# Up projection of a feed-forward block: seven products of half blocks in place of eight for nineteen of twenty-two pairs of tiles

## The chip, the core and the metric

The kernel runs on one core of a Trainium2 chip. TensorE (PE) multiplies, PEld is its weight load, VectorE is DVE, ScalarE is ACT, GpSimd is POOL, and SyncE (SP) issues nearly all DMAs. The metric is the device time of one execution in microseconds; a lower time is better. Before the change the median of three runs is 3589.12 us (3586.46 to 3591.07).

## What is computed

The reference is one layer of an encoder, applied to two batches of 1024 tokens by 1024 features with the same weights. Its last part, which the change touches for the second batch, is a gated feed-forward block with a convolution of width three along the tokens:

```python
D_MODEL = 1024; SEQ = 1024; D_FF = 2816
def _conv_ffn(x, l, prm):
    h = x @ prm['ffn_up'][l]                       # (1024, 1024) @ (1024, 5632)
    cw = prm['conv_w'][l]
    h = cw[0] * _shift_prev(h) + cw[1] * h + cw[2] * _shift_next(h) + prm['conv_b'][l]
    gate, up = jnp.split(h, 2, axis=-1)
    return (jax.nn.gelu(gate, approximate=False) * up) @ prm['ffn_down'][l]

x = _layer_norm(ALPHA * x + _conv_ffn(x, l, prm), prm['ln2_g'][l], prm['ln2_b'][l])
```

Everything before it in the layer (the input projection, the two head groups, the output projection and its norm) is the same before and after.

## The kernel before

Each fp32 operand is split into a high part (`hi`, a rounded copy that ACT makes) and a low part (`lo`, the difference, by POOL for weights and by DVE for activations), and a product of two operands is three matmuls: hi by hi, hi by lo, lo by hi. A matmul multiplies a 128x128 block of weights with 512 tokens and adds to one bank of PSUM.

The normalised input of the feed-forward block stands transposed in `xh` and `xl` (feature block k of 8, 1024 tokens). `phase_f1` runs over 22 pairs j. A pair is two tiles of 128 output features, the gate tile `j` and the up tile `KF + j`. For one tile `weights` loads 512 KB of weights (SP, tile `w`), splits them (`split`: two ACT copies at line 248, four POOL subtractions at line 251 into a second `w`), and `dense` issues 2 halves of the tokens x 8 feature blocks x 3 matmuls (lines 264 to 266) into a PSUM tile `d` of two banks; there are two such tiles, taken in turn. Then ACT applies the middle tap and the bias (line 1068), DVE adds the other two taps (lines 1069 and 1071). With both tiles of a pair there, ACT applies the gelu (line 1074), DVE multiplies (line 1075), and ACT and DVE split the result into `h` (lines 307 and 308).

For the second batch the first half of the tokens of `h` stays in SBUF, in the tile `h`; the second half goes to DRAM and is read back. `phase_f2` multiplies `h` with the down projection: for each half of the tokens and each half of the output features, 22 blocks k x 4 tiles of tokens x 3 matmuls (`dense_t`, lines 288 to 290).

All engines execute in the order of their own queue and wait for semaphores. A scheduler makes these orders from the order of the code, at build time. The tiles come from pools with a fixed number of buffers (`BUFS`: 4 of `w`, 2 of `whi`, 7 of `t`; 2 of the PSUM tile `d`); an instruction that takes a buffer over waits for the last reader of its former content.

## Time and profile before

| what | value |
|---|---|
| median of three runs | 3589.12 us |
| the profiled execution's own time | 3581.8 us |
| its span in the profile | 3580.1 us |
| TensorE busy over the span | 3207.8 us (90%) |
| DVE, ACT and POOL busy over the span | 54%, 38%, 36% |
| up projection of the second batch | about 2838 to 3314 us of the span |
| down projection of the second batch and the last norm | from 3314 us to the end |

The page gives the busy time of each engine over the whole program. The two stages of the table are read from windows of the trace, from timelines of single engines, and from the groups of instructions by line.

### The profile page before, as it was taken

Reading aid. Unit: us, or ns where it says so; the run is one execution under the profiler, and the core shown is the slowest. Engines: PE = TensorE matmul, PEld = TensorE weight load, DVE = VectorE, ACT = ScalarE, POOL = GpSimd, SP = SyncE. Lnnn points to the kernel's source line nnn. Section 1 sums busy time; section 2 is a strip of 40 time slices with the busy share of each in tenths; the row PEclk is TensorE's granted clock in tenths of the full one; section 3 lists DMA queues with packets and bytes.
Section 4 is the critical chain, followed back from the end, with each engine's and each line's share of the span. In section 5 each row is a group of like instructions: output and inputs, shape, how many; then the busy total and the mean of one; then the engine's idle time right before and its main releaser. Section 6 shows DMA issues by size and latency. Waiting matters only on the chain.

```text
span 3580.1 us, 56015 instructions
## 1 busy us (share of the span) xinstructions
PE 3207.8 (90%) x21477; PEld 2543.4 (71%) x21477; DVE 1948.3 (54%) x3550; ACT 1360.1 (38%) x2318; POOL 1299.1 (36%) x1387
## 2 busy tenths in 40 slices
PE   5787877998999986798999999988997899999997
PEld 4566655776778874666778787766875688888876
DVE  6377873345557866888544434356685733333022
ACT  3243432443245643454344343324454433332222
POOL 5265441101322345544211112363352622222464
PEclk9898888998999987888999999989999999999999
DMA  5568875443455655676643336566662322222652
GB/s 163 164 205 228 217 193 142 139 111 112 132 170 162 218 199 152 169 184 163 143 128 111 111 109 219 195 225 196 189 193 86 112 78 76 71 71 73 227 173 86
DMA packets 603359, 545.59 MB, mean 152 GB/s; under 512 B 205340, under 2 KB 477964, under 8 KB 603092
## 3 DMA queue, kind: packets, MB, share of 16 engines
q1 hardware_dynamic: 536532, 508.44, 46.9%
q10 hardware_dynamic: 66560, 33.56, 3.9%
q8 instruction: 171, 2.80, 0.3%
q14 instruction: 96, 0.79, 0.1%
HBM read 361.49 MB, written 180.39 MB: 151 GB/s over the span
## 4 chain that ended last, share of the span: by engine, by line
PE 61%; DVE 14%; DMA 10%; issue 4%; ACT 4%; POOL 4%; SPq 3%; ACTq 0%; DVEq 0%; POOLq 0%
PE d L264 10%; PE d L266 10%; PE d L265 10%; PE s L722 8%; PE d L288 5%; PE d L289 5%; PE d L290 5%; SPq L79 3%; DVE Ntmp L619 2%; DVE N L621 2%; POOL w L251 2%; PE s L917 1%; PE s L918 1%; PE s L942 1%; DMA ab<-AB 1%
## 5 line engine op out<-in xcount | busy, mean ns | idle before, releaser
L251 POOL TENSOR_TENSOR w<-w,whi 128x256 fp32r<-128x256 f32 (+1 forms) x800 | 758.6, 976 | 1271.8 <-ACT whi L248 1117.8
L264 PE MATMUL d<-xh,whi 128*128 128x512 f32 (+1 forms) x2112 | 858.7, 407 | 15.0 <-DVE t L399 6.0
L266 PE MATMUL d<-xh,w 128*128 128x512 f32 (+1 forms) x2112 | 848.5, 402 | 2.3 <-POOL w L251 2.3
L265 PE MATMUL d<-xl,whi 128*128 128x512 f32 (+1 forms) x2112 | 845.4, 400 | 0.6 <-DVE xl L308 0.6
L248 ACT ACTIVATE whi<-w 128x512 fp32r<-128x512 f32 (+1 forms) x536 | 308.0, 622 | 730.1 <-PE d L290 259.5
L264 PEld LDWEIGHTS d<-xh,whi 128*128 128x128 f32 (+1 forms) x2112 | 405.9, 192 | 107.1 <-issue 7.5
L266 PEld LDWEIGHTS d<-xh,w 128*128 128x128 f32 (+1 forms) x2112 | 405.5, 192 | 98.9 <-POOL w L251 3.7
L265 PEld LDWEIGHTS d<-xl,whi 128*128 128x128 f32 (+1 forms) x2112 | 405.7, 192 | 93.3 <-issue 3.3
L1069 DVE SCALAR_TENSOR_TENSOR t<-d,cols,t 128x1023 f32<-128x1023 f32 x88 | 112.8, 1282 | 444.4 <-ACT t L1068 444.4
L288 PE MATMUL d<-whi,xh 128*128 128x512 f32 x640 | 261.8, 416 | 38.2 <-DVE t L1049 21.7
L289 PE MATMUL d<-w,xh 128*128 128x512 f32 x640 | 262.9, 411 | 5.8 <-POOL w L251 5.8
L290 PE MATMUL d<-whi,xl 128*128 128x512 f32 x608 | 247.2, 407 | 0.0
L1049 DVE SCALAR_TENSOR_TENSOR t<-t,d 128x512 f32<-128x512 f32 x112 | 72.7, 680 | 259.5 <-PE d L290 252.4
L926 ACT ACTIVATE e<-e,ms 128x1024 f32<-128x1024 f32 x128 | 146.9, 1148 | 125.4 <-DVE ms L924 105.8
L933 POOL TENSOR_SCALAR e<-e,ms 128x512 f32<-128x512 f32 x128 | 87.6, 698 | 264.5 <-DVE ms L931 122.6
L288 PEld LDWEIGHTS d<-whi,xh 128*128 128x128 f32 x640 | 124.8, 195 | 75.9 <-DVE t L1049 14.1
L289 PEld LDWEIGHTS d<-w,xh 128*128 128x128 f32 x640 | 125.4, 196 | 36.4 <-POOL w L251 8.9
L722 PE MATMUL s<-G,BK 64*128 64x128 f32 x1024 | 110.6, 306 | 35.5 <-DMA Tt<-td 17.8
L290 PEld LDWEIGHTS d<-whi,xl 128*128 128x128 f32 x608 | 118.2, 194 | 27.7
L917 PE MATMUL s<-k,qh 128*128 128x512 f32 x256 | 113.3, 444 | 25.5 <-DVE ms L920 16.5
L619 DVE TENSOR_TENSOR Ntmp<-N 128x30 f32<-128x30 f32 (+14 forms) x240 | 115.6, 482 | 36.5 <-DMA N<-abd 31.5
L737 DVE TENSOR_TENSOR G<-s,ms 64x256 f32<-64x256 f32 x128 | 53.5, 418 | 144.3 <-PE s L722 143.1
(226 smaller groups left out, 5748.9 us busy)
## 6 DMA issues: line engine op xcount, KB each, us to landing
w<-in_ffn_up SPq DMA_DIRECT2D x88, 512.0 KB
w<-in_ffn_down SPq DMA_DIRECT2D x88, 512.0 KB
h<-t SPq DMA_DIRECT2D x66, 512.0 KB
ab<-AB ACTq DMA_DIRECT2D x64, 512.0 KB
w<-in_w_in SPq DMA_DIRECT2D x58, 512.0 KB
G<-ab SPq DMA_DIRECT2D x128, 128.0 KB
BK<-ab SPq DMA_DIRECT2D x64, 256.0 KB
w<-in_w_out SPq DMA_DIRECT2D x32, 512.0 KB
```

What stands on the lines that cost most here:

```text
L248: nc.scalar.activation(out=hi[:, s], in_=w[:, s], func=AF.Copy)
L251: nc.gpsimd.tensor_tensor(out=lo[:, s], in0=w[:, s], in1=hi[:, s].bitcast(F32), op=ALU.subtract)
L264: nc.tensor.matmul(o, wh, rh, start=first, stop=False)
L265: nc.tensor.matmul(o, wh, rl, start=False, stop=False)
L266: nc.tensor.matmul(o, wl, rh, start=False, stop=last)
L288: nc.tensor.matmul(out[i], lh, wh, start=k == ks[0], stop=False)
L289: nc.tensor.matmul(out[i], lh, wl, start=False, stop=False)
L290: nc.tensor.matmul(out[i], ll, wh, start=False, stop=k == ks[-1])
L619: nc.vector.tensor_tensor(out=tv, in0=N[:, 0:j, j : j + 1].to_broadcast([P, j, w]), in1=N[:, j : j + 1, j + 1 : 32].to_broadcast([P, j, w] ...
L722: last = self.nc.tensor.matmul(*args, **kw)
L917: nc.tensor.matmul(pp, q_[0], k_[c][:, ks], start=True, stop=False)
L926: nc.scalar.activation(out=e_, in_=e_, func=AF.Exp, bias=ms[:, 2 + c : 3 + c], accum_out=ms[:, 4 + c : 5 + c])
```

## The change

For the pairs 3 to 21 of the second batch the two tiles of a pair are computed together. The weights of a pair are four half blocks: `a11` and `a12` are the feature blocks 0 to 3 and 4 to 7 of the gate tile, `a21` and `a22` those of the up tile. The tokens are two halves as well, so that four quarter results (`c11`, `c12` for the gate tile, `c21`, `c22` for the up tile) are two products of half blocks each, eight in all. Winograd's form of Strassen's scheme needs seven products of sums instead. Each of these is 4 feature blocks x 3 matmuls.

* `right` makes the sums of the activations once, in tiles `T1`, `T2`, `T4` (and a fourth sum over the second half of the tokens of blocks 0 to 3 in `xh` and `xl` themselves), during the pairs 0 to 2, which still take eight products.
* `seven` loads a pair's weights, makes four sums `s1` to `s4` on DVE, splits seven half blocks (a copy on ACT and a subtraction on POOL each), and issues the seven products. Their order on TensorE is enforced (`issue_after(self.turn)`): s1, a11, then the last product (a22) of the pair before, then s2, a12, s4, s3.
* Between the products three copies on ACT move partial results (`es` from `e`; `c12` from `c11`; `c21` from `c12`, lines 1183, 1184, 1187), and two additions on DVE add `es` (line 1152).
* All of `h` of the second batch goes to DRAM, and `phase_f2` reads all of it back, into the buffers of the sums and of `xh` and `xl`, as half as large transfers.

The core of the diff (parts of `phase_f1` that only move into functions are left out):

```diff
-            def pre(k):
+            def pre(k, n):
+                if n:
+                    return
...
-            self.dense_t(w, 512 * n, ks, lhs, range(4 * g, 4 * g + 4), put, n, pre if n == 0 else None, last and n == 1)
...
+            self.dense_t(w, 512 * n, ks, lhs, range(4 * g, 4 * g + 4), put, n, lambda k: pre(k, n), last and n == 1)
...
+        def eight(m):
+            ws = self.weights(I["ffn_up"][0], m * P, KT)
+            pp = self.dpsum()
+            self.dense(pp, ws, rhs, (0, 1), KT)
+            return pp
...
+        def gated(j, gate, up):
+            nc.scalar.activation(out=gate, in_=gate, func=AF.Gelu)
+            nc.vector.tensor_tensor(out=up, in0=gate, in1=up, op=ALU.mult)
             for half in range(2):
-                stay = keep is not None and half == 0
-                o = keep[:, j] if stay else self.dt("t", F32R, shape=(P, 2, 512))
-                self.hilo(gu[1][:, 512 * half : 512 * half + 512], o[:, 0], o[:, 1])
-                if not stay:
-                    self.ld(out=S["h"][j][half], in_=o)
-
-    def phase_f2(self, b, out, keep=None):
+                o = self.dt("t", F32R, shape=(P, 2, 512))
+                self.hilo(up[:, 512 * half : 512 * half + 512], o[:, 0], o[:, 1])
+                self.ld(out=S["h"][j][half], in_=o)
+
...
+        if tl is None:
+            for j in range(KF):
+                gated(j, *(conv(eight(m), m) for m in (j, KF + j)))
+            return None
+        right, early = self.right(tl), 3
+        for j in range(early):
+            pps = [eight(m) for m in (j, KF + j)]
+            if j == 0:
+                next(right)
+            if j == early - 1:
+                blocks = next(right)
+            gated(j, conv(pps[0], j), conv(pps[1], KF + j))
+        self.turn = None
+        last = None
+        for j in range(early, KF):
+            this = self.seven(tl, j, blocks)
+            next(this)
+            if last:
+                gated(j - 1, gate, conv(next(last), KF + j - 1))
+            gate, last = conv(next(this), j), this
+        gated(KF - 1, gate, conv(next(last), 2 * KF - 1))
+        return blocks
+
+    def right(self, tl):
+
+
+        nc = self.nc
+        xh, xl = self.xT
+        block = lambda a, b: [tuple(x[:, 4 * a + k, 512 * b : 512 * b + 512] for x in (xh, xl)) for k in range(4)]
+        T = [tl(f"T{i}", dt=F32R, shape=(P, 4, 2, 512)) for i in (1, 2, 4)]
+        op = lambda out, a, b, o: nc.vector.tensor_tensor(out=out, in0=a, in1=b, op=o)
+        at = lambda a, b, k: [x[:, 4 * a + k, 512 * b : 512 * b + 512].bitcast(F32) for x in (xh, xl)]
+        one = lambda: tl("S", 4)
+        for k in range(4):
+            b11, b12, b21, b22 = (at(a, b, k) for a in range(2) for b in range(2))
+            t1, u = one(), one()
+            op(t1, b12[0], b11[0], ALU.subtract)
+            nc.gpsimd.tensor_tensor(out=u, in0=b12[1], in1=b11[1], op=ALU.subtract)
+            op(t1, t1, u, ALU.add)
+            for n, b in ((0, None), (1, b22), (2, b21)):
+                if b:
+                    op(t1, b[0], t1, ALU.subtract)
+                    op(t1, t1, b[1], ALU.add)
+                self.hilo(t1, T[n][:, k, 0], T[n][:, k, 1])
+        yield
+        for k in range(4):
+            b12, b22 = at(0, 1, k), at(1, 1, k)
+            t3, u = one(), one()
+            op(t3, b22[0], b12[0], ALU.subtract)
+            nc.gpsimd.tensor_tensor(out=u, in0=b22[1], in1=b12[1], op=ALU.subtract)
+            op(t3, t3, u, ALU.add)
+            self.hilo(t3, *(x[:, k, 512:1024] for x in (xh, xl)))
+        of = lambda t: [(t[:, k, 0], t[:, k, 1]) for k in range(4)]
+
+        yield [of(T[0]), block(0, 0), of(T[2]), of(T[1]), block(1, 0), block(1, 1), block(0, 1)]
+
+    def seven(self, tl, j, right):
+
+
+        nc, w = self.nc, self.I["ffn_up"][0]
+        raw = []
+        for m in (j, KF + j):
+            raw.append(self.dt("w", shape=(P, 8, P)))
+            self.ld(out=raw[-1], in_=w[:, m * P : (m + 1) * P].rearrange("(k p) c -> p k c", p=P))
+        a11, a12, a21, a22 = (r[:, 4 * h : 4 * h + 4] for r in raw for h in range(2))
+        op = lambda out, a, b, o: nc.vector.tensor_tensor(out=out, in0=a, in1=b, op=o)
+        s1, s2, s3, s4 = (tl("S", 4, shape=(P, 4, P)) for _ in range(4))
+        op(s1, a21, a22, ALU.add)
+        op(s2, s1, a11, ALU.subtract)
+        op(s4, a12, s2, ALU.subtract)
+        op(s3, a11, a21, ALU.subtract)
+        ha, la = self.dt("whi", F32R, shape=(P, 8, P)), self.dt("w", F32R, shape=(P, 8, P))
+        left = {}
+        for name, a in (("s1", s1), ("a11", a11), ("s2", s2), ("a12", a12), ("s4", s4), ("s3", s3), ("a22", a22)):
+            if name in ("a11", "a12"):
+                hi, lo = (x[:, 0:4] if name == "a11" else x[:, 4:8] for x in (ha, la))
+            else:
+                hi, lo = (tl("o", 16, F32R, (P, 4, P)) for _ in range(2))
+            nc.scalar.activation(out=hi, in_=a, func=AF.Copy)
+            nc.gpsimd.tensor_tensor(out=lo, in0=a, in1=hi.bitcast(F32), op=ALU.subtract)
+            left[name] = hi, lo
+
+        def product(o, a, b, first):
+            (ah, al), b = left[a], right[b]
+            for k in range(4):
+                for x, (l, r) in enumerate(((ah, 0), (ah, 1), (al, 0))):
+                    with self.tc.issue_after(self.turn) if self.turn and k == x == 0 else nullcontext():
+                        ins = nc.tensor.matmul(o, l[:, k], b[k][r], start=first and k == x == 0, stop=k == 3 and x == 2,
+                                               skip_group_check=True)
+            self.turn = ins.ins
+
+        e, p1, p2 = self.spsum(), self.dpsum(), self.dpsum()
+        c11, c12, c21, c22 = (p[:, 512 * h : 512 * h + 512] for p in (p1, p2) for h in range(2))
+        product(e, "s1", 0, True)
+        product(c11, "a11", 1, True)
+        es = self.dt("t")[:, 0:512]
+        nc.scalar.copy(out=es, in_=e)
+        nc.scalar.copy(out=c12, in_=c11)
+        yield
+        product(c12, "s2", 3, False)
+        nc.scalar.copy(out=c21, in_=c12)
+        product(c11, "a12", 4, False)
+        product(c12, "s4", 5, False)
+        op(c12, c12, es, ALU.add)
+        product(c21, "s3", 6, False)
+        op(c22, c21, es, ALU.add)
+        yield p1
+        product(c21, "a22", 2, False)
+        yield p2
...
+            if slots is None:
+                parts = [(range(k0, min(k0 + 8, KF)), {k: own[8 * ((3 * j + k0 // 8) % 2) + k % 8] for k in range(k0, min(k0 + 8, KF))})
                          for k0 in range(0, KF, 8)]
             else:
-                parts = [(range(KF), {k: keep[:, k] if j == 0 else slots[k] if k < 16 else keep[:, k - 16] for k in range(KF)})]
-            for i, (ks, at) in enumerate(parts):
+                at = {(jj, k): slots[(KF * jj + k) % len(slots)] for jj in range(2) for k in range(KF)}
+                parts = [(range(KF), {k: at[j, k] for k in range(KF)})]
+
+            def fill(jj, k):
+                for x in range(2):
+                    self.ld(out=at[jj, k][x], in_=S["h"][k][jj][:, x])
...
+                def pre(k, n):
+                    if n == 0 and k == 6:
                         rs.update(self.rows(j, S["x1"]))
-                    if k == 21 and j == 0:
+                    if n == 0 and k == 21 and j == 0:
                         gb.extend(self.gb(I["ln2_g"][0], I["ln2_b"][0]))
-                    if keep is None or j == 1 and k >= 16:
-                        self.ld(out=at[k], in_=S["h"][k][j])
-                    elif j == 0 and 4 <= k < 20:
-                        self.ld(out=slots[k - 4], in_=S["h"][k - 4][1])
+                    if slots is None:
+                        if n == 0:
+                            self.ld(out=here[k], in_=S["h"][k][j])
+                    elif j == 0 and n == 0:
+                        for kk in range(4) if k == 0 else ():
+                            fill(0, kk)
+                        if k + 4 < KF:
+                            fill(0, k + 4)
+                    elif j == 0:
+                        fill(1, k)
...
-            h = pool.tile([P, KF, 2, 512], F32R, name="h")
-            self.phase_f1(1, h)
-            self.phase_f2(1, y1, h)
+            def tl(tag, bufs=1, dt=F32, shape=(P, 512)):
+                return pool.tile(list(shape), dt, name=self.nm(tag), tag=tag, bufs=bufs)
+
+            right = self.phase_f1(1, tl)
+            self.phase_f2(1, y1, [at for block in right for at in block])```

Nothing moves ahead of the second batch's up projection. In it the queues of three engines change as follows; the pieces are from the middle, where each pair's pattern repeats.

On DVE, the up projection of the second batch; one pair is five rows. `d` is a PSUM tile, `cols` holds the taps, `t` and `h` are results:

```order
L1069 SCALAR_TENSOR_TENSOR t_26474<-d_26425,cols,t_26474 128x1023
L1071 SCALAR_TENSOR_TENSOR t_26474<-d_26425,cols,t_26474 128x1023
L1075 TENSOR_TENSOR t_26474<-t_26411,t_26474 128x1024
L308 TENSOR_TENSOR h<-t_26474,h 128x512
L308 TENSOR_TENSOR t_26482<-t_26474,t_26482 128x512
L1069 SCALAR_TENSOR_TENSOR t_26545<-d_26496,cols,t_26545 128x1023
L1071 SCALAR_TENSOR_TENSOR t_26545<-d_26496,cols,t_26545 128x1023
```

The same place now. `S` are the sums of the weights of pair 8, `w_26631` and `w_26633` its two loads, `d_26372` the gate tile and `d_26373` the up tile of pair 6, `t_26398` its `es`, `t_26423` a result of pair 5:

```order
L308 TENSOR_TENSOR t_26419<-t_26413,t_26419 128x512
L308 TENSOR_TENSOR t_26423<-t_26413,t_26423 128x512
L1152 TENSOR_TENSOR S_26635<-w_26633 128x512
L1152 TENSOR_TENSOR S_26636<-S_26635,w_26631 128x512
L1152 TENSOR_TENSOR S_26638<-w_26631,S_26636 128x512
L1152 TENSOR_TENSOR S_26637<-w_26631,w_26633 128x512
L1152 TENSOR_TENSOR d_26372<-d_26372,t_26398 128x512
L1073 SCALAR_TENSOR_TENSOR t_26478<-d_26372,cols,t_26478 128x1023
L1152 TENSOR_TENSOR d_26373<-d_26373,t_26398 128x512
L1075 SCALAR_TENSOR_TENSOR t_26478<-d_26372,cols,t_26478 128x1023
L1073 SCALAR_TENSOR_TENSOR t_26562<-d_26373,cols,t_26562 128x1023
```

Four sums of a later pair now stand ahead of the addition that completes a gate tile, and the addition of the up tile stands between the two taps of the gate tile.

On ACT, the same stretch before:

```order
L1068 ACTIVATE t_26813<-d_26764,cols 128x1024
L1074 ACTIVATE t_26813<-t_26813 128x1024
L248 ACTIVATE whi_26953<-w_26951 128x512 x2
L1068 ACTIVATE t_26876<-d_26827,cols 128x1024
L307 ACTIVATE h<-t_26876 128x512
L307 ACTIVATE t_26884<-t_26876 128x512
```

And now, from the two copies of pair 8's `a11` and `a12` on; `o` are split weights, `s_26520` is `e` of pair 7, `d_26521` and `d_26522` are the gate and up tiles of pair 7:

```order
L1165 ACTIVATE whi_26643<-w_26631 128x512 x2
L1165 ACTIVATE o_26645<-S_26635 128x512
L1072 ACTIVATE t_26478<-d_26372,cols 128x1024
L1165 ACTIVATE o_26651<-S_26636 128x512
L1165 ACTIVATE o_26657<-S_26638 128x512
L1183 COPY t_26547<-s_26520 128x512
L1080 ACTIVATE t_26478<-t_26478 128x1024
L1184 COPY d_26521<-d_26521 128x512
L1165 ACTIVATE o_26661<-S_26637 128x512
L1072 ACTIVATE t_26562<-d_26373,cols 128x1024
L1165 ACTIVATE o_26665<-w_26633 128x512
L1187 COPY d_26522<-d_26521 128x512
```

The copy of line 1187 now stands behind the middle tap of the up tile before it. On POOL only the subtractions of the weights remain (line 1166), seven of 512 columns for a pair in place of eight of 256, in the order of ACT's copies.

On TensorE, at a seam between two products, with the semaphores that a row waits for. Before, from one tile to the next:

```order
L264 MATMUL d_26157<-xh,whi_26149 128x512 [waits DVE_49,Activation_49]
L265 MATMUL d_26157<-xl,whi_26149 128x512
L266 MATMUL d_26157<-xh,w_26150 128x512 [waits Pool_49]
L264 MATMUL d_26157<-xh,whi_26149 128x512
L265 MATMUL d_26157<-xl,whi_26149 128x512
```

Now, the end of the product of s2 and the start of that of a12, of pair 6:

```order
L1174 MATMUL d_26372<-T_3598_25532,o_26354 128x512
L1174 MATMUL d_26372<-T_3598_25532,o_26353 128x512 x2
L1174 MATMUL d_26372<-T_3598_25532,o_26354 128x512
L1174 MATMUL d_26372<-xh,whi_26345 128x512 [waits Activation_49]
L1174 MATMUL d_26372<-xl,whi_26345 128x512
L1174 MATMUL d_26372<-xh,w_26346 128x512
```

The first matmul of a12 waits for ACT: the count that it waits for is that of the copy at line 1187, although it writes `c11`, the other bank of the tile, and that copy reads `c12`.

## Rows read from the trace of the kernel before

**Rows 1.** The page: busy time, share of the span, instructions.

```profile
PE 3207.8 (90%) x21477; PEld 2543.4 (71%) x21477; DVE 1948.3 (54%) x3550; ACT 1360.1 (38%) x2318; POOL 1299.1 (36%) x1387
```

**Rows 2.** Windows: stretch, its us, busy us (instructions) by engine, clock, DMA.

```profile
2940.00:2960.00 20.00, 20.00 (x89) 16.43 (x88) 7.65 (x7) 6.71 (x9) 5.69 (x8) 1.00 0.25 79
...
3320.00:3340.00 20.00, 19.38 (x86) 15.50 (x85) 1.59 (x3) 5.77 (x10) 9.23 (x8) 1.00 1.01 388
3340.00:3400.00 60.00, 59.89 (x265) 49.31 (x264) 3.67 (x6) 12.68 (x22) 27.97 (x23) 1.00 0.50 171
```

**Rows 3.** Timeline of ACT, up projection: start, duration, line, count, [idle before <- releaser].

```profile
2941.67 1.19 ACT L1068 ACTIVATE t<-d,cols 128x1024 f32<-128x1024 f32 x1
2946.79 0.63 ACT L307 ACTIVATE h<-t 128x512 fp32r<-128x512 f32 x1 [3.93 <-DVE t L1075]
2947.32 0.62 ACT L307 ACTIVATE t<-t 128x512 fp32r<-128x512 f32 x1
...
2952.66 1.19 ACT L1068 ACTIVATE t<-d,cols 128x1024 f32<-128x1024 f32 x1
2956.58 1.06 ACT L1074 ACTIVATE t<-t 128x1024 f32<-128x1024 f32 x1 [2.73 <-DVE t L1071]
...
2963.64 1.19 ACT L1068 ACTIVATE t<-d,cols 128x1024 f32<-128x1024 f32 x1
```

**Rows 4.** Timeline of DVE, the same pair and the next.

```profile
2945.53 1.22 DVE L1075 TENSOR_TENSOR t<-t,t 128x1024 f32<-128x1024 f32 x1
2947.45 0.69 DVE L308 TENSOR_TENSOR h<-t,h 128x512 fp32r<-128x512 f32 x1 [0.70 <-ACT h L307]
2948.06 0.68 DVE L308 TENSOR_TENSOR t<-t,t 128x512 fp32r<-128x512 f32 x1
2953.88 1.28 DVE L1069 SCALAR_TENSOR_TENSOR t<-d,cols,t 128x1023 f32<-128x1023 f32 x1 [5.13 <-ACT t L1068]
2955.20 1.28 DVE L1071 SCALAR_TENSOR_TENSOR t<-d,cols,t 128x1023 f32<-128x1023 f32 x1
```

**Rows 5.** Timeline of all engines at the end of the up projection.

```profile
3313.68 0.39 PE L265 MATMUL d<-xl,whi 128*128 128x512 f32 x1
3313.91 0.39 PE L266 MATMUL d<-xh,w 128*128 128x512 f32 x1
...
3314.16 1.15 ACT L248 ACTIVATE whi<-w 128x512 fp32r<-128x512 f32 x2 [4.95 <-PE d L265]
...
3314.92 2.55 POOL L251 TENSOR_TENSOR w<-w,whi 128x512 fp32r<-128x512 f32 x2 [8.43 <-ACT whi L248]
```

**Rows 6.** Timeline of DVE where attention, norms and output projection run side by side.

```profile
2613.71 0.68 DVE L334 TENSOR_TENSOR t<-t,t 128x512 f32<-128x512 f32 x1
2614.42 0.69 DVE L335 TENSOR_TENSOR t<-t,t 128x512 f32<-128x512 f32 x1
...
2616.85 0.68 DVE L308 TENSOR_TENSOR aTl<-s,aTh 128x512 fp32r<-128x512 f32 x1
2617.85 1.44 DVE L334 TENSOR_TENSOR t<-t,t 128x512 f32<-128x512 f32 x1 [0.32 <-ACT t L333]
2619.32 1.63 DVE L335 TENSOR_TENSOR t<-t,t 128x512 f32<-128x512 f32 x1
```

**Rows 7.** Timeline of POOL, the same stretch.

```profile
2616.20 2.54 POOL L251 TENSOR_TENSOR w<-w,whi 128x512 fp32r<-128x512 f32 x2
2618.70 1.71 POOL L334 TENSOR_TENSOR t<-t,t 128x512 f32<-128x512 f32 x1
```

**Rows 8.** Timeline of PE, two pauses; windows right behind them, columns as above.

```profile
470.77 1.85 PE L580 MATMUL s<-AB 64*64 64x64 f32 x32 [2.40 <-DVE AB L576]
...
928.70 0.68 PE L722 MATMUL s<-A,Tt 64*64 64x64 f32 x16 [1.95 <-DVE v L857]
...
471.00:477.80 6.80, 6.80 (x81) 5.50 (x78) 6.59 (x12) 1.27 (x2) 2.22 (x2) 0.50 0.67 160
...
928.80:935.60 6.80, 6.16 (x66) 4.61 (x67) 4.70 (x12) 2.57 (x4) 2.57 (x4) 1.00 0.40 117
```

More of the change, by code (lines that the diff above doesn't have):

```diff
@@ L1083, in phase_f2, with conv @@
[L1083 removed]
+        def eight(m):
[3 more added lines that the diff above has]
+            return pp
+        def conv(pp, m):
+            o = self.dt("t")
+            nc.scalar.activation(out=o, in_=pp, func=AF.Identity, scale=self.cw[1][:, m : m + 1], bias=self.cb[:, m : m + 1])
+            nc.vector.scalar_tensor_tensor(out=o[:, 1:T], in0=pp[:, 0 : T - 1], scalar=self.cw[0][:, m : m + 1],
+                                           in1=o[:, 1:T], op0=ALU.mult, op1=ALU.add)
+            nc.vector.scalar_tensor_tensor(out=o[:, 0 : T - 1], in0=pp[:, 1:T], scalar=self.cw[2][:, m : m + 1],
+                                           in1=o[:, 0 : T - 1], op0=ALU.mult, op1=ALU.add)
+            return o
@@ L1084, in phase_f2 @@
+    def phase_f2(self, b, out, slots=None):
         nc, I, S = self.nc, self.I, self.st[b]
         gb = []
-        slots = [x[:, k0 + k].rearrange("p (a t) -> p a t", a=2) for k0 in (0, 4) for x in self.xT for k in range(4)]
+        own = [x[:, k0 + k].rearrange("p (a t) -> p a t", a=2) for k0 in (0, 4) for x in self.xT for k in range(4)]
         for j in range(2):
```

26 lines of the change are left out of this document (5 added, 21 removed).

## The prediction

> **What bounds the kernel now.** I read the page first: TensorE is busy for 90% of the span [rows 1]. Then the stage. In the up projection of the second batch PE is busy for the whole of a window at the full 2.4 GHz, while DVE works 7.65 of 20 us, ACT 6.71 and POOL 5.69 [rows 2]. So this stage is bound by the number of matmuls: the middle tap of a tile starts 10.99 us after that of the tile before, and 21.97 us after that of the same tile of the pair before [rows 3]. A pair is 96 matmuls, which makes 0.229 us for one, and the two neighbouring starts agree [rows 5]. The other engines wait for PE most of the time [rows 3, 4]; what they do costs nothing as long as it ends within a pair. Next I read how long one step of each takes and how fast one engine wakes another, because the change puts ACT, POOL and DVE between products of one pair.
>
> **What is removed.** A product of half blocks is 12 matmuls, 12 x 0.229 = 2.75 us. Seven in place of eight give 84 x 0.229 = 19.23 us for a pair in place of 21.97. For 19 pairs this is 52 us, if PE never waits. The rest of this part asks whether it waits.
>
> **The wait ahead of a12.** On PE the order is a22 of the pair before, s2, a12. By the order of the queues the first matmul of a12 waits for ACT's copy of `c12` into `c21` (line 1187). That copy takes over the up tile of the pair before, so it waits until DVE has read that tile for its second tap, and that can start only when a22 is done. The chain, from the end of a22:
> PE to ACT 0.25 (the last matmul starts one slot of 0.23 before the end, runs 0.39, and ACT starts 0.09 later [rows 5]); the copy of s3's weights, which stands ahead in ACT's queue, 0 to 0.55 (two such starts lie 0.53 apart [rows 3]; its buffer comes free a little before a22 ends, so part of it is hidden); middle tap, both other taps and the wake of ACT from 2952.66 to 2956.58, 3.92 [rows 3, 4]; the copy itself 0.62, the nearest row being the copy of 512 columns [rows 3]; ACT to PE about 0.1. That is 4.9 to 5.4; I take 5.2. The product of s2 covers 2.75 of it. PE then waits 2.1 to 2.7 us, I take **2.4**, in every pair from the fourth on. No row of before shows ACT or DVE writing PSUM, so the copy may be 0.3 us cheaper or dearer than its nearest row; that lies in the range.
>
> **The wait ahead of a11.** The product of a11 is the first that writes the gate tile of the next pair, and it takes over the gate tile of this one. From the end of s4 alone: 0.25 to wake DVE, `c12 + es` 0.68, 0.1 to ACT, middle tap 1.19, first tap 1.32, the addition of the up tile, which stands in between, 0.64, second tap 1.28, 0.1 to PE: 5.6 us. The products of s3 and e cover 5.5. So PE waits about 0.1, if DVE is free when s4 ends.
> It is not. Its queue has, ahead of `c12 + es`: the gating product and the two subtractions of the pair before and four sums of weights two pairs ahead. Counted from the start of a12: the second tap of the up tile ends 0.8 before; product 1.23, 0.7 until ACT has copied, two subtractions 1.3, four sums (two depend on each other: 0.71 a step [rows 6]) 2.7. With small gaps that ends at 5.25, half a microsecond ahead of s4's result at 5.75. But POOL gets the weights of the same later pair just then: ACT copies `a11` and `a12` when a12 has freed their buffer, at 2.75, and POOL starts 0.7 later and has three subtractions in a row (the two halves and s1).
> What this costs is in the trace. A DVE instruction that reads two tensors from SBUF takes 0.68 or 0.69 alone, and 1.44 and 1.63 while POOL works on tensors of its own; POOL's takes 1.71 there in place of 1.27 (2.54 for two); an addition with one operand in PSUM keeps its 0.68 beside the same POOL instruction [rows 6, 7]. The two take turns, one whole instruction each. Each of three POOL instructions then holds up one sum by about 1.2: DVE comes to `c12 + es` at 5.25 + 3.6 = 8.9, 3.1 us late, and PE waits 0.1 + 3.1 = **3.2** ahead of a11. Bounds: 0.1 (no meeting at all) and 4.5 (a fourth meeting, or sums that start late because their weights, whose buffer POOL frees last, land late).
> The Trainium skill, page SBUF — State Buffer, section "SBUF: two separate sides", states the rule that speaks against this change: a DVE instruction with two SBUF inputs and a GpSimd instruction that reads SBUF share one pair of ports as an exclusive lock, and the one that comes first keeps it for its whole instruction. The rows above agree. By the rule each meeting would cost a whole POOL instruction, 1.29 in place of my 1.2, which adds 16 x 3 x 0.09 = 4 us to the sum; if the two shared bandwidth, the wait would stay near its lower bound.
>
> **A pair then takes** 19.23 + 2.4 + 3.2 = 24.8 us, 2.9 more than now. Sums for a later pair exist for 16 of these; 16 x 2.9 = +46. The last two pairs have the first wait alone: 19.23 + 2.4 = 21.6, -1 together.
>
> **The start.** The sums of the activations are 48 DVE instructions with two SBUF operands, some 31 us, in the first three pairs, where DVE has about 14 us of each 22 free; that fits. But twelve of them stand ahead of the first tile's first tap, with three POOL subtractions that meet them: 12 x 0.65 + 3 x 1.2 = 11 us, in which the first PSUM tile is not released. The third tile needs it. PE has one tile of work meanwhile, begun during the norms; I take a loss of 8 (4 to 12). When the first pair of seven begins, none of its weights are split ahead: ACT has about 13 copies and a middle tap in its queue before the first partial result, some 8.4 us, and DVE's gating meets POOL, against 5.5 us of products; the same again before the next copy. I take 10 (3 to 14).
>
> **The down projection** has the same matmuls. All of `h` is now written and read back, 11.5 MB for each half of the tokens. The half that was kept comes in during the first quarter, some 60 us, with 5.8 MB of weights and some rows: about 20 MB, 330 GB/s. The DMAs have moved 388 GB/s in one window and 171 in the next [rows 2]. The first eight blocks can be loaded before the up projection ends. I take 0, with 10 as the bound if the transfers of half the size move less.
>
> **Sum:** 46 - 1 + 8 + 10 = +63 us. Against the profiled execution, 3580.1 us of span and 3581.8 of its own time, this is 3645; that one lies 7.3 below the median of the runs, so the median becomes 3589.1 + 63 = **3652**.
>
> **Rivals.** *No meeting.* POOL's start slips behind the four sums, or DVE goes first. Then a pair takes 19.23 + 2.4 + 0.1 to 0.4, about 21.9, as now; with half of the start terms, +9, and -1 for the last pairs the time is about 3595. For it: the two queues start within a microsecond of each other. Against it: POOL has three instructions in a row, so a shift of one moves one meeting only.
> *The gain shows.* The copy at line 1187 does not hold PE, or is done within s2, and DVE is in time: 52 less 18 for the start, about 3555. Against it: the chain from a22 is 4.9 us even with its lowest terms, and s2 is 2.75.
> *The clock falls.* After a pause of 2.40 us PE ran at 1.2 GHz, 0.50 of the full clock, in the next window; after one of 1.95 it stayed at 1.00 [rows 8]. A pair has two pauses, of 2.4 and 3.2. If 5 us behind each run at half the clock, a pair loses up to 2 x 2.5 us. A slower a12 also moves POOL's work behind DVE's sums, which gives back part of the second wait; with half given back, 16 x 2.5 = 40 more: 3692. In the forecast the two cancel.
>
> **How the numbers follow.** Forecast (both waits, 3625 to 3680) 0.70; clock 0.17; no meeting 0.08; gain 0.05. A measurement of this kernel can tell 0.2%, some 7 us, from no change. Forecast and clock are slower, 0.87; no meeting is within 0.2%, 0.08; gain is faster, 0.05. The range leaves out the gain, most of "no meeting" and the upper part of "clock": 3598 to 3700.
>
> **What the changed profile would show.** Middle taps of gate tiles 24 to 26 us apart; PE idle ahead of a12 for some 2.4 us with ACT's line 1187 as releaser, and ahead of a11 for some 3 us with DVE's second tap; DVE's line 1152 sums of 1.5 us and more beside POOL's line 1166; a fallen clock in the slices. If the taps are 21.9 apart and the sums take 0.7, the meeting was wrong; if PE is busy through a pair and the taps are 19.2 apart, both waits were.

## The result: 2.2% slower, with the waits where they were expected

| what | before | after |
|---|---|---|
| median of the runs, same chip | 3587.79 us (4 runs) | 3665.35 us (4 runs) |
| ratio, 95% interval | | 1.0221 (1.0203 to 1.0240) |
| profiled execution, its span | 3581.8, 3580.1 us | 3666.35, 3664.6 us |

The forecast was 3652 with a range of 3598 to 3700; the time lies 13 us above it. PE has less to do and the others more, as the first line of the page after shows beside [rows 1]:

```profile
PE 3196.3 (87%) x21249; PEld 2517.4 (69%) x21249; DVE 2110.0 (58%) x3712; ACT 1435.5 (39%) x2448; POOL 1400.1 (38%) x1376
```

**Where the time went.** The two spans differ by 84.5 us, but 8.2 of that lie ahead of the change. The same pause of PE in the last norm, 2.90 us behind `rs`, which no edit touches, ends at 2837.23 before and at 2845.43 after (a row of PE's timeline in each kernel, before and then after):

```profile
2837.23 1.09 PE L345 MATMUL s<-ident,rs 128*128 128x128 f32 x4 [2.90 <-DVE rs L335]
```

```profile
2845.43 0.87 PE L345 MATMUL s<-ident,rs 128*128 128x128 f32 x3 [2.90 <-DVE rs L335]
```

So 76.3 us belong to the change, which agrees with the medians (77.6). A gate tile's middle tap (line 1068 before, 1072 after) marks each pair. Here are PE's two long waits in the stage of the pairs of seven (2940 to 3396 us), by releaser (us in total, times, longest):

```profile
PE d L1174 <- ACT d L1187: 39.1, 18, 2.2
PE d L1174 <- DVE t L1075: 32.1, 16, 3.2
```

These are the two waits of the forecast, with the releasers that it named. In the windows PE, 20.00 of 20 us at work before [rows 2], is now busy for 82 to 87% (stretch, its us, busy us of PE, PEld, DVE, ACT, POOL, clock, DMA share, GB/s):

```profile
3000.00:3060.00 60.00, 52.18 (x203) 40.88 (x201) 30.05 (x28) 23.93 (x35) 20.93 (x15) 0.91 0.21 71
3100.00:3160.00 60.00, 49.39 (x204) 38.94 (x204) 31.56 (x29) 24.91 (x37) 23.61 (x17) 0.97 0.21 70
```

One pause of each kind, on PE's timeline with the releaser in brackets; then DVE's and POOL's timelines from a12's start on, one fence each:

```profile
3160.06 0.50 PE L1174 MATMUL d<-xh,whi 128*128 128x512 f32 x1 [2.19 <-ACT d L1187]
...
3174.56 0.47 PE L1174 MATMUL d<-xh,whi 128*128 128x512 f32 x1 [3.21 <-DVE t L1075]
```

```profile
3161.48 1.29 DVE L308 TENSOR_TENSOR t<-t,t 128x512 fp32r<-128x512 f32 x2 [0.70 <-ACT t L307]
3163.86 1.59 DVE L1152 TENSOR_TENSOR S<-w 128x512 f32<-128x512 f32 x1 [1.08 <-DMA w<-in_ffn_up]
3165.54 1.61 DVE L1152 TENSOR_TENSOR S<-S,w 128x512 f32<-128x512 f32 x1
3167.26 1.60 DVE L1152 TENSOR_TENSOR S<-w,S 128x512 f32<-128x512 f32 x1
3168.78 0.68 DVE L1152 TENSOR_TENSOR S<-w,w 128x512 f32<-128x512 f32 x1
3169.39 0.69 DVE L1152 TENSOR_TENSOR d<-d,t 128x512 f32<-128x512 f32 x1
```

```profile
3163.61 3.00 POOL L1166 TENSOR_TENSOR w<-w,whi 128x512 fp32r<-128x512 f32 x2 [3.90 <-ACT whi L1165]
3166.57 1.74 POOL L1166 TENSOR_TENSOR o<-S,o 128x512 fp32r<-128x512 f32 x1
```

Three POOL instructions meet three sums; each of those sums takes 1.6 us, the fourth, alone, 0.68. The completion of the gate tile (`c12 + es`), forecast 8.9 us behind a12's start, begins 9.33 behind it (3169.39 less 3160.06): the first sum also waited 1.08 us for its weights to land.

**The pairs.** Middle taps of gate tiles, from ACT's timeline (every second row, the up tile's, is left out):

```profile
3095.48 1.21 ACT L1072 ACTIVATE t<-d,cols 128x1024 f32<-128x1024 f32 x1 [1.53 <-DVE d L1152]
...
3119.85 1.21 ACT L1072 ACTIVATE t<-d,cols 128x1024 f32<-128x1024 f32 x1 [1.53 <-DVE d L1152]
...
3144.95 1.21 ACT L1072 ACTIVATE t<-d,cols 128x1024 f32<-128x1024 f32 x1 [3.78 <-DVE d L1152]
...
3170.11 1.21 ACT L1072 ACTIVATE t<-d,cols 128x1024 f32<-128x1024 f32 x1 [3.64 <-DVE d L1152]
...
3196.84 1.21 ACT L1072 ACTIVATE t<-d,cols 128x1024 f32<-128x1024 f32 x1 [3.83 <-DVE d L1152]
```

The steps are 24.37, 25.10, 25.16 and 26.73 us, where they were 21.97 [rows 3]. From the fifth of the 16 pairs on there are only these three lengths, and they are three fates of the clock. With no fall a pair takes 25.1. Where the clock fell behind the pause ahead of a12 (7 to 9 of its matmuls 0.43 us apart in place of 0.229), a pair takes 24.4. Where it fell behind the pause ahead of a11, nothing is given back and a pair takes 26.7. The first four pairs take 25.49, 27.81, 25.65 and 25.90: the second and the fourth have a fall behind a11, and in the first three the weights land later (DVE waits 1.2 to 1.3 us for them ahead of its sums, in the others 0.8 to 1.1). The mean of the 16 periods from 2941.69 to 3346.29 is 25.29.

The pause ahead of a11 is 3.15 to 3.24 us in all seven cases behind a fast a12 in these 16 pairs, and 0.8 to 1.0 in 8 of 9 behind a slow one. A slow a12 does more than use up part of that pause. From the start of a12 to the middle tap of its gate tile it is 10.0 to 10.1 us where a12 is fast (3160.06 to 3170.11), and 9.2 to 9.4 in 8 of 9 cases where it is slow (3110.59 to 3119.85), although a slow a12 takes 1.6 us longer. So what sets the time there is not PE but DVE's queue, and behind a slow a12 two sums meet POOL and not three. One such pair, DVE's sums and PE's pause ahead of a11:

```profile
3114.19 0.69 DVE L1152 TENSOR_TENSOR S<-w 128x512 f32<-128x512 f32 x1 [0.88 <-DMA w<-in_ffn_up]
3114.97 0.69 DVE L1152 TENSOR_TENSOR S<-S,w 128x512 f32<-128x512 f32 x1
3115.77 1.73 DVE L1152 TENSOR_TENSOR S<-w,S 128x512 f32<-128x512 f32 x1
3117.42 1.78 DVE L1152 TENSOR_TENSOR S<-w,w 128x512 f32<-128x512 f32 x1
```

```profile
3124.31 0.47 PE L1174 MATMUL d<-xh,whi 128*128 128x512 f32 x1 [0.94 <-DVE t L1075]
```

A fall is read from PE's rows: two matmuls of a slow a12, which start 0.43 us apart, and two of one at full speed.

```profile
3111.18 0.63 PE L1174 MATMUL d<-xl,whi 128*128 128x512 f32 x1
3111.61 0.63 PE L1174 MATMUL d<-xh,w 128*128 128x512 f32 x1
...
3160.40 0.40 PE L1174 MATMUL d<-xl,whi 128*128 128x512 f32 x1
3160.63 0.39 PE L1174 MATMUL d<-xh,w 128*128 128x512 f32 x1
```

### The profile page after: what moved, and what is told of

Its sections match the earlier page's. It is cut to its first block, busy times and chain, and to the rows that moved or that the text cites. A ratio compares the mean times of both kernels' runs of the same rounds, so it can differ in the third digit from the quotient of the medians.

```text
span 3664.6 us, 56251 instructions
## 1 busy us (share of the span) xinstructions
PE 3196.3 (87%) x21249; PEld 2517.4 (69%) x21249; DVE 2110.0 (58%) x3712; ACT 1435.5 (39%) x2448; POOL 1400.1 (38%) x1376
## 4 chain that ended last, share of the span: by engine, by line
PE 54%; DVE 21%; DMA 10%; issue 5%; ACT 4%; POOL 3%; SPq 3%; ACTq 0%; DVEq 0%; POOLq 0%
PE s L722 7%; PE d L264 6%; PE d L265 6%; PE d L266 6%; PE d L288 5%; PE d L289 5%; PE d L290 5%; PE d L1174 5%; SPq L79 3%; DMA w<-in_ffn_up 2%; DVE Ntmp L619 2%; DVE N L621 2%; DVE S L1152 2%; DVE t L1073 2%; DVE t L1075 2%
## 5 line engine op out<-in xcount | busy, mean ns | idle before, releaser
L251 POOL TENSOR_TENSOR w<-w,whi 128x256 fp32r<-128x256 f32 (+2 forms) x648 | 655.3, 1037 | 962.3 <-ACT whi L248 789.2
L264 PE MATMUL d<-xh,whi 128*128 128x512 f32 (+1 forms) x1504 | 622.5, 414 | 22.6 <-ACT whi L248 6.9
L265 PE MATMUL d<-xl,whi 128*128 128x512 f32 x1504 | 614.0, 408 | 0.6 <-DVE xl L308 0.6
L266 PE MATMUL d<-xh,w 128*128 128x512 f32 x1504 | 611.9, 407 | 2.3 <-POOL w L251 2.3
L248 ACT ACTIVATE whi<-w 128x512 fp32r<-128x512 f32 x460 | 264.0, 621 | 560.2 <-PE d L290 238.7
L264 PEld LDWEIGHTS d<-xh,whi 128*128 128x128 f32 (+1 forms) x1504 | 293.6, 195 | 94.9 <-issue 14.5
L266 PEld LDWEIGHTS d<-xh,w 128*128 128x128 f32 x1504 | 293.2, 195 | 72.6 <-POOL w L251 3.6
L265 PEld LDWEIGHTS d<-xl,whi 128*128 128x128 f32 x1504 | 293.8, 195 | 67.4 <-issue 3.0
L1073 DVE SCALAR_TENSOR_TENSOR t<-d,cols,t 128x1023 f32<-128x1023 f32 x88 | 112.7, 1281 | 319.1 <-ACT t L1072 319.0
L1166 POOL TENSOR_TENSOR o<-S,o 128x512 fp32r<-128x512 f32 x76 | 106.6, 1409 | 159.6 <-ACT o L1165 159.5
L722 PE MATMUL s<-G,BK 64*128 64x128 f32 x1024 | 110.8, 306 | 36.6 <-DMA Tt<-td 18.3
L1174 PE MATMUL d<-xh,whi 128*128 128x512 f32 x152 | 72.6, 478 | 74.4 <-ACT d L1187 41.3
```

The lines of the kernel that those rows point to most:

```text
L248: nc.scalar.activation(out=hi[:, s], in_=w[:, s], func=AF.Copy)
L251: nc.gpsimd.tensor_tensor(out=lo[:, s], in0=w[:, s], in1=hi[:, s].bitcast(F32), op=ALU.subtract)
L264: nc.tensor.matmul(o, wh, rh, start=first, stop=False)
L265: nc.tensor.matmul(o, wh, rl, start=False, stop=False)
L266: nc.tensor.matmul(o, wl, rh, start=False, stop=last)
L722: last = self.nc.tensor.matmul(*args, **kw)
```

## The experiments

The kernel before ran beside each group of kernels on the same chip; its medians there were 3582.75 (beside `copy_behind_a12`, `sums_on_pool`, `no_activation_sums` and `eight_throughout`), 3592.16 (beside `pool_half_instructions`, `third_psum_tile`, `third_tile_new_turn` and `third_tile_new_turn_sums_pool`) and 3590.03 (beside `pauses_filled`, `third_tile_in_use_before` and `four_pairs_of_eight_all_fixes`). Ratios are to those, with 95% intervals.

### What holds a12

```diff
-        nc.scalar.copy(out=c21, in_=c12)
         product(c11, "a12", 4, False)
+        nc.scalar.copy(out=c21, in_=c12)
```

> The copy of c12 into c21 is written behind the product of a12, so a12 no longer stands behind it; the order of the products is the same. Theory (a12 waits only for that copy): the pause of 2.19 us ahead of a12, 39.1 us in 18 pairs, is gone. The copy now stands ahead of s4, which has to wait for it: the chain from a22 of 4.9 us then lies beside s2 and a12 (5.5 us), so the pause ahead of s4 is 1 to 2 us (copy 0.57 and two wakes at least, since the copy now waits for a12). The scheduler also puts the sums of weights behind the completion of the gate tile, so the pause ahead of a11 should be near 1. A pair takes 19.2 + 1.5 + 1 = 21.7 to 22.5 in place of 25.3: 16 x 3 = 48 less, 3610 to 3625 us. Rival (a12 waits for its weights or its bank): its pause stays at 2.2, and the time at 3655 to 3670.

Measured: 3612.29 us, ratio 1.0077 (1.0062 to 1.0092). PE's waits in the middle of the stage (2945 to 3280 us):

```profile
PE d L1174 <- ACT d L1188: 22.3, 15, 1.5
PE d L1174 <- ACT t L1183: 13.7, 14, 1.1
```

The pause ahead of a12 is gone, one of 1.49 us ahead of s4 takes its place, and about 1 us stands ahead of a11, now behind another copy of ACT. A pair takes 22.2 us, and the clock is 1.00 in three windows of 60 us between 3000 and 3260. The theory holds: a12 waited for that copy and for nothing else that lasts as long. Which share of the 52 us (by the ratios, 1.0221 and 1.0077) comes from the copy alone is not separated: the scheduler also moved two of the four sums of weights behind the gate tile's completion, and of the four only one now meets POOL (1.18 us, the others 0.68 to 0.69), which shortens the second pause. No run takes the pause ahead of a12 away and leaves DVE's queue and the tiles as they were.

### What makes DVE late

```diff
+        po = lambda out, a, b, o: nc.gpsimd.tensor_tensor(out=out, in0=a, in1=b, op=o)
-        op(s1, a21, a22, ALU.add)
-        op(s2, s1, a11, ALU.subtract)
-        op(s4, a12, s2, ALU.subtract)
-        op(s3, a11, a21, ALU.subtract)
+        po(s1, a21, a22, ALU.add)
+        po(s2, s1, a11, ALU.subtract)
+        po(s4, a12, s2, ALU.subtract)
+        po(s3, a11, a21, ALU.subtract)
```

> The four sums of weights of a pair are made by POOL in place of DVE. Theory (DVE's sums and POOL's subtractions take turns, and that makes DVE late for the completion of the gate tile): the pause ahead of a11 falls from 2.0 on average to 0.3 or less; that ahead of a12 stays at 2.2. POOL then works 11 x 1.28 = 14 us of a pair, which fits. A pair takes 19.2 + 2.2 + 0.2 = 21.6, or 23.2 where the clock falls at a12: 16 x 2.1 to 3.7 less than now, 3606 to 3632 us. Rival (the chain from s4 through both taps holds PE, whatever DVE does before): the pause ahead of a11 stays between 0.9 and 3.2 and the time above 3650.

Measured: 3618.24 us, 1.0097 (1.0077 to 1.0116). In the same stretch PE's waits are one line; the pause ahead of a11 is gone altogether:

```profile
PE d L1175 <- ACT d L1188: 33.3, 15, 2.2
```

Here the fall of the clock can be read alone, since no second pause gives it back. ACT's rows for gate tiles:

```profile
3000.12 1.21 ACT L1072 ACTIVATE t<-d,cols 128x1024 f32<-128x1024 f32 x1 [0.27 <-DVE d L1152]
...
3023.47 1.21 ACT L1072 ACTIVATE t<-d,cols 128x1024 f32<-128x1024 f32 x1 [0.27 <-DVE d L1152]
...
3046.82 1.21 ACT L1072 ACTIVATE t<-d,cols 128x1024 f32<-128x1024 f32 x1 [0.27 <-DVE d L1152]
...
3070.19 1.21 ACT L1072 ACTIVATE t<-d,cols 128x1024 f32<-128x1024 f32 x1 [0.27 <-DVE d L1152]
...
3091.92 1.21 ACT L1072 ACTIVATE t<-d,cols 128x1024 f32<-128x1024 f32 x1 [0.27 <-DVE d L1152]
```

A pair takes 23.35 us here in 11 of 16 cases, and 21.73 (3070.19 to 3091.92) where the clock does not fall: a fall costs 1.6 us.

### Whether the two take turns by whole instructions

```diff
-            nc.gpsimd.tensor_tensor(out=lo, in0=a, in1=hi.bitcast(F32), op=ALU.subtract)
+            for k in (0, 2):
+                nc.gpsimd.tensor_tensor(out=lo[:, k : k + 2], in0=a[:, k : k + 2], in1=hi[:, k : k + 2].bitcast(F32), op=ALU.subtract)
```

> POOL's subtraction of a half block of weights is two instructions of 256 columns in place of one of 512; the rest is as in the changed kernel. Theory (DVE and POOL take turns by whole instructions): a sum of DVE that meets POOL waits for half as long an instruction and takes 1.1 to 1.4 us in place of 1.6 to 1.8; the pause ahead of a11 shrinks by about a third (32 us in all to some 20), the time to 3645 to 3660 us. Rival (both work at once and share the bandwidth): a sum beside POOL stays at 1.6 to 1.8 and the time at 3665 or a little above, since POOL has twice the instructions.

Measured: 3640.40 us, 1.0137 (1.0119 to 1.0155), some 30 us less than the changed kernel by the ratios, with the same work, and 5 us below the range that was expected. DVE's four sums of one pair, beside POOL's instructions of half the length:

```profile
3146.96 1.01 DVE L1152 TENSOR_TENSOR S<-w 128x512 f32<-128x512 f32 x1 [0.98 <-DMA w<-in_ffn_up]
3148.06 1.05 DVE L1152 TENSOR_TENSOR S<-S,w 128x512 f32<-128x512 f32 x1
3149.22 1.05 DVE L1152 TENSOR_TENSOR S<-w,S 128x512 f32<-128x512 f32 x1
3150.19 1.23 DVE L1152 TENSOR_TENSOR S<-w,w 128x512 f32<-128x512 f32 x1
```

```profile
3146.68 4.18 POOL L1167 TENSOR_TENSOR w<-w,whi 128x256 fp32r<-128x256 f32 x4 [3.77 <-ACT whi L1165]
```

A sum takes 1.0 to 1.2 in place of 1.6 to 1.8, the pause ahead of a11 is 2.1 in place of 3.2, and a pair 24.0 in place of 25.1. Shared bandwidth would have left the sums as long as they were. The Trainium skill, page SBUF — State Buffer, section "SBUF: two separate sides", has the rule of the lock that is held for a whole instruction; the trace agrees (1.6 beside an instruction of 512 columns, 1.05 beside one of 256).

### What the start costs

```diff
-        for k in range(4):
-            b11, b12, b21, b22 = (at(a, b, k) for a in range(2) for b in range(2))
...
-            self.hilo(t3, *(x[:, k, 512:1024] for x in (xh, xl)))
...
-        yield [of(T[0]), block(0, 0), of(T[2]), of(T[1]), block(1, 0), block(1, 1), block(0, 1)]
+        yield [block(0, 1), block(0, 0), block(1, 1), block(1, 0), block(1, 0), block(1, 1), block(0, 1)]
```

> The sums of the activations are left out; the seven products take the blocks themselves, so the output is another. Theory (the sums on DVE delay the first tap of the first tile and fill DVE's queue up to the first pair of seven): 8.2 us at the start and some of the 14 us lost at the entry to the first pair of seven are gone, the pairs behind are as now: 3649 to 3657 us. Rival (the losses come from loads and from the entry of seven alone): less than 3 us change, 3662 or more.

Measured: 3648.88 us, 1.0180 (1.0153 to 1.0206), some 15 us less than the changed kernel by the ratios. Counted so that the norm's pause of 2.90 us ends at 2837.23 in each, the gate tile of pair 3 is reached at 2923.8 (2921.26 + 2.56) in place of 2933.5 (2941.69 - 8.2), 9.7 us earlier, and the wait of the third tile for a first tap, 4.3 us after the change, is not there. Before, that tile is reached at 2908.7. Of the 24.8 us lost up to there, 2.8 are the order alone (a gate tile now comes behind five products of 2.75, before behind 10.99 us), and 12 remain: the entry itself, where PE waits 5.1 us ahead of s2 for ACT's first copy between banks, behind ACT's copies of weights that were not split ahead. The pairs behind are not as they were: the 16 of them take 412.4 us in place of 404.6, with four of 26.7 where the changed kernel has two, so that from the norm's pause to the end this profile is only 7 us shorter (812.0 and 819.2 us). The intervals of the two ratios overlap, so of the two numbers the 9.7 us of the trace are the better measure of the start.

```diff
-        right, early = self.right(tl), 3
-        for j in range(early):
+        right = self.right(tl)
+        for j in range(KF):
             pps = [eight(m) for m in (j, KF + j)]
             if j == 0:
                 next(right)
...
-        for j in range(early, KF):
-            this = self.seven(tl, j, blocks)
...
+        return next(right)
```

> All 22 pairs of the second batch take eight products; the sums of the activations are still made (their last part at the end), and all of h still goes through DRAM. Theory (the pairs of seven, with the entry to them, hold 66 of the 78 us): what is left is 8.2 at the start and 1.6 in the down projection: 3595 to 3602 us, with pairs of 21.97. Rival (the way of h through DRAM, or the sums, cost more than they show): above 3605.

Measured: 3597.64 us, 1.0039 (1.0024 to 1.0054), 15 us above before. All pairs of the middle take 22.0 us again, but the wait for the first tap is there:

```profile
PE d L264 <- DVE t L1075: 6.2, 1, 6.2
```

From the norm's pause to the end this profile is 15.0 us longer than that of before. Up to the last up tile it has lost 8.9, as at the start of the changed kernel; the other 6.1 follow, where this kernel makes its last sums and PE waits 4.2 us for a copy of weights at the seam. In the changed kernel that last part is 2.5. So the way of `h` through DRAM costs at most these 2.5, and the pairs of seven hold most of the loss.

### Whether the pauses make the clock fall, and what that costs

```diff
+        def fill(n):
+            z = self.spsum()
...
+                    ins = nc.tensor.matmul(z, left["s1"][0][:, i % 4], right[0][i % 4][0], start=i == 0, stop=i == n - 1)
+            self.turn = ins.ins
...
+        fill(13)
         product(c11, "a11", 1, True)
...
+        fill(9)
         product(c11, "a12", 4, False)
```

> The changed kernel with PE kept at work in its pauses: 13 matmuls ahead of a11 and 9 ahead of a12 (3.0 and 2.1 us) into a bank that nobody reads; everything else in the same order. Theory (the clock falls to 1.2 GHz because of the pauses, and costs more than it gives back): the clock stays at full speed over the stage, the 245 slow matmuls of the pairs are gone, and a pair takes 19.2 + 2.2 + 3.2 = 24.6 to 24.9 in place of 25.3: 5 to 14 us less than the changed kernel's 3665, 3650 to 3660 us, though PE does 22 x 19 matmuls more. Rival (the slow matmuls come from something else than the pauses, or what the fall costs is all given back): slow matmuls remain, or the time is 3665 or more.

Measured: 3665.43 us, 1.0219 (1.0192 to 1.0245): the changed kernel's time, with 418 matmuls more. The first half of the theory holds, and the time is not the one that was expected:

```profile
3100.00:3160.00 60.00, 58.45 (x254) 47.01 (x254) 31.25 (x31) 25.51 (x38) 22.53 (x18) 1.00 0.23 74
```

The clock stays at 1.00: the pauses were what made it fall. What the falls cost, this run does not show. Its pairs take 25.0 to 25.6 us, as long as the changed kernel's without a fall (25.1), but they are made of other parts: DVE waits 3.5 us for its weights to land, where it waited 1.08, and then only one of its sums meets POOL (1.75 us, the others 0.69), so that the two lengths agree by coincidence. Probably the extra matmuls hold buffers longer and so delay the loads. The cost of the falls is read from the pairs of the changed kernel: 24.4 and 26.7 around 25.1, 3 us in all over the 16 pairs. PE's rows have some 100 slow matmuls there, not the 245 that were expected.

### Taking the waits away

In the five kernels of this part the tiles of a pair rotate over three PSUM tiles. Where a pair of seven is the first to use the third tile (`third_psum_tile` and the two runs with the new order that follow), the output for the second batch is another, and the record does not show at which sum it goes astray; the instructions are those described. In `third_tile_in_use_before` and the last run the pairs of eight use the third tile first, and the output is the layer's. The times with and without that agree (3582.30 and 3580.71 us).

```diff
+        self.psx.close()
+        with self.tc.tile_pool(name="pe", bufs=1, space=PSUM) as self.pe, self.tc.tile_pool(name="px", bufs=1, space=PSUM) as self.ps, self.tc.tile_pool(name="f1", bufs=1) as pool:
...
+    def tri(self):
+        self.n3 = getattr(self, "n3", 0) + 1
+        if self.n3 % 3 == 0:
+            return self.pe.tile([P, 1024], F32, name=self.nm("d"), tag="d")
+        return self.dpsum()
...
-        e, p1, p2 = self.spsum(), self.dpsum(), self.dpsum()
+        e, p1, p2 = self.spsum(), self.tri(), self.tri()
```

> The up and gate tiles of a pair of seven rotate over three PSUM tiles in place of two (two banks that e had to itself); order and engines are the same. Theory (both pauses are waits for a PSUM tile that is taken over): a11 finds a tile that has long been read, its pause is gone; the copy into c21 finds its tile free, so it waits for s2 alone, and a12 behind it for 0.25 + 0.57 + 0.1, about 1 us. A pair takes 20.2 to 20.6, at the full clock, and the time is 3665 - 32 - 21 - 31 for the clock = 3581, between 3572 and 3592 us. Rival (the sums and splits of weights are late by themselves, and only looked like a wait for a tile): PE waits ahead of s1 or a11 for weights, a pair stays above 22 and the time above 3610.

Measured: 3580.71 us, 0.9974 (0.9963 to 0.9985). Over the same stretch:

```profile
PE d L1181 <- ACT d L1194: 16.4, 16, 1.0
```

Both long waits were for a tile that is taken over, with the sums and the splits of weights on the same engines as before; what is left is the copy between s2 and a12, 1.03 us, and a pair takes 20.57.

```diff
-            pps = [eight(m) for m in (j, KF + j)]
+            pps = [eight(m, self.tri) for m in (j, KF + j)]
```

> As the run third_psum_tile, but the three pairs of eight use the three tiles in turn too, so that each bank has held a whole product before the pairs of seven add to copies in it. Theory: the first tap no longer holds up the third tile of the stage, so the wait of 4.3 us at the start goes, and the activation sums, as many as before, show at the entry to the first pair of seven in its place: pairs of 20.5 as in that run, the time within 5 us of its 3581. Rival (the wait at the start was a loss of its own): 5 us or more less.

Measured: 3582.30 us, 0.9978 (0.9961 to 0.9994). The wait at the start is gone, and PE waits 9.2 us for the split of s1 at the entry: the sums of activations cost the same wherever they show.

With the third tile, the order of the products is changed next:

```diff
-        product(e, "s1", 0, True)
         product(c11, "a11", 1, True)
+        nc.scalar.copy(out=c12, in_=c11)
+        product(e, "s1", 0, True)
...
-        nc.scalar.copy(out=c12, in_=c11)
-        yield
         product(c12, "s2", 3, False)
         nc.scalar.copy(out=c21, in_=c12)
+        yield
```

> With three PSUM tiles the order of the products is a11, s1, s2, then a22 of the pair before, a12, s4, s3, so that each of the two copies between banks has a whole product beside it. Theory (what is left after the third tile is the copy ahead of a12): a pair takes 19.2 to 19.8 us, 18 x 1 less than with the third tile alone: 3555 to 3572 us, faster than the kernel before. Rival (DVE or ACT becomes the bound at this pace): a pair above 20.5, no gain over the third tile alone.

Measured: 3554.85 us, 0.9902 (0.9883 to 0.9921). A pair takes 19.26 us (84 times 0.229 are 19.24), and PE has no idle time in the windows:

```profile
3100.00:3160.00 60.00, 60.00 (x263) 48.93 (x262) 45.73 (x42) 31.35 (x47) 33.04 (x23) 1.00 0.34 113
```

The edit of `sums_on_pool` is added to that:

> As the run with three PSUM tiles and the new order, and the four sums of weights are made by POOL. Theory (DVE and POOL no longer meet in the sums, and the entry to the first pair of seven gets shorter): pairs of 19.2 to 19.4, the entry some 3 us shorter: 5 to 10 us less than without, 3545 to 3565 us. Rival (POOL with 11 x 1.28 = 14 us a pair and its waits for ACT's copies becomes late): PE waits for POOL's line 1167 ahead of s1 or s4, and the time is 3565 or more.

Measured: 3553.86 us, 0.9899 (0.9879 to 0.9919). The two intervals are the same, so the 5 to 10 us were not found: once PE no longer waits for DVE, the meeting no longer shows in the time.

The last kernel adds a fourth pair of eight, the third tile from the first pair on, and activation sums without POOL:

```diff
-        right, early = self.right(tl), 3
+        right, early = self.right(tl), 4
...
-            nc.gpsimd.tensor_tensor(out=u, in0=b12[1], in1=b11[1], op=ALU.subtract)
+            nc.vector.tensor_tensor(out=u, in0=b12[1], in1=b11[1], op=ALU.subtract)
```

> Three PSUM tiles from the first pair on, the new turn (a11, s1, s2, a22 of the pair before, a12, s4, s3), the weight sums on POOL, the activation sums on DVE alone, and four pairs of eight in place of three. Theory (the losses were the waits for tiles, the meeting of DVE and POOL, and the entry before the sums are done): 18 x 2.75 = 49 us less work, some 10 us lost at the entry: 36 to 44 us less than before, 3545 to 3556 us. Rival (the entry costs the same 14 us wherever it stands, and one more pair of eight loses 2.7): no faster than the 3554 of the run with the new turn and the sums on POOL.

Measured: 3545.75 us, 0.9883 (0.9858 to 0.9907): 44 us below the kernel before, as expected, and with the output of the layer. By the medians it is the fastest of all, but its interval overlaps those of the two kernels before it. In its profile the way from the norm's pause to the end takes 700.7 us, in place of 742.9 before and 706.7 in the run with the new order and the sums on POOL: one execution of each. Of the 49.7 us that 18 pairs of 19.21 save, 5 are lost up to the last up tile, at the start and the entry, and 2.5 behind it. Three things were changed at once, so what the fourth pair of eight gains is not separated.

## Why the prediction was right, step by step

| step | forecast | measured |
|---|---|---|
| start, to the gate tile of pair 2 | +8 | +8.2 (2903.10 - 2886.73 - 8.2) |
| entry, with the shorter end of the last pair | +10 | +12.0 |
| 16 pairs | +46 | +53.1 (404.6 - 16 x 21.97) |
| last two pairs | -1 | +0.8 |
| down projection and last norm | 0 | +2.5 |
| sum | +63 | +76.5 |

**The wait ahead of a12** was right in place, releaser and size: 2.4 forecast, 2.19 idle. Taking the copy from in front of a12 removed it, and giving the copy a free tile left 1.03. Its price is another matter. In the sum the two waits are added; but while DVE is late, DVE's queue sets when the gate tile is complete, and a12 may run 1.6 us longer without delaying it. PE's wait ahead of a12 holds a pair by itself only once DVE is in time, as in `sums_on_pool` (21.73).

**The wait ahead of a11** was right too where the clock did not fall: 3.2 forecast, 3.15 to 3.24 measured, with three meetings in the pair. That the number fits so well is in part luck. The four sums take 5.5 us (3163.86 to 3169.39), where 2.7 + 3.6 were reckoned: a meeting costs 0.94, not 1.2 and not a whole POOL instruction. But they begin 1.2 later than reckoned, since their weights land late, and that was named only as an upper bound. The mean of the wait over the 16 pairs is only 2.0, because a slow a12 shortens it. The forecast had put what a fall costs against what it gives back and let the two cancel. The mechanism that it named, POOL's work moving behind DVE's sums, is in the rows; that they cancel was a choice, and the pairs show that they nearly do (24.4 and 26.7 around 25.1).

**The terms that were mis-sized.** A pair without a fall takes 25.1, not 24.8. PE's idle time in the rows starts where the last matmul ends, 0.16 behind its slot (0.39 less 0.23 [rows 5]), and the first matmul behind a pause takes longer (0.47 and 0.50). So 2.19 and 3.2 of idle cost 5.9 us together (25.1 less 19.24), where 5.6 were reckoned: over 16 pairs some 4 of the 7 us. The other 3 are a balance: the first four pairs and the two of 26.7 add 7.7, and the seven of 24.4 take back 4.8. The entry was 2 us dearer, and the last two pairs lost 1.6 to one fall of the clock. The start came out at +8.2 by another sum than the forecast's. PE waits there for 4.3 us, not 8; the rest is matmuls at 1.2 GHz, for which the forecast had no term: 11 behind that wait, and seven more than before in the first tile.

**The rivals.** "No meeting" fell: two or three meetings stand in nearly every pair of the changed kernel; they shrink with POOL's instructions and vanish when the sums leave DVE. "The gain shows" fell in this kernel, but its number was near: with the waits taken away the time is 3546 to 3555, where the rival had 3555. "The clock falls" was right that the clock falls, and wrong that half of the cost would be kept.

## What to carry to other kernels

Fewer products pay only if the engine that sets the pace never waits for what connects them: here 52 us of saved matmuls became a loss of 76, through two waits for PSUM tiles that are taken over (97 us over 16 pairs, 25.29 less 19.24 each, the falls of the clock among them) and some 20 us at the start and the entry. Before a partial result is moved between banks, give each copy a whole product beside it and each pair a tile that has long been read; that changed the order of seven products and the use of two banks that `e` could spare, and no arithmetic. Where two engines are late in the same stretch, ask which of them sets the end of it: time taken from the other gains nothing. Where two engines take turns at a port, the length of one instruction is the price of a meeting, so a long one on the engine that is not urgent is split or moved.

## What the hardware showed beyond the forecast

The clock does not fall behind every pause of the same length. Behind the 2.19 us ahead of a12 it fell in 9 of 17 pairs of the changed kernel, and behind the 3.2 ahead of a11 in 3 of 7; with 2.25 in each pair (`sums_on_pool`) in 11 of 16. It also fell behind one pause of 1.90, where in the kernel before it stayed at 1.00 behind 1.95 [rows 8]. With a pause of 1.49 and one of about 1 in each pair (`copy_behind_a12`) the windows show 1.00. A fall in a pair made mostly 7 to 9 matmuls run at 1.2 GHz and cost PE 1.6 us. An ACT copy of 512 columns from PSUM to PSUM takes 0.57 us, less than the 0.62 of ACT's copies of 512 columns between SBUF tiles, and a DVE addition that reads and writes PSUM 0.69, as much as one in SBUF without POOL beside it.
